# Gate and up projections of a two-layer decoder trunk as 2x2 block products: seven half-width products in place of eight

## The chip, the core and the metric

The kernel runs on one core of a Trainium2 chip. The metric is the device time of one execution in microseconds (us), lower is better. Before the change it is 1854.85 us (median of 3 runs, 1853.87 to 1855.31).

## What is computed

The program is a trunk of two layers over 512 positions of width 1024, all in float32. Each layer is a feed-forward network (FFN), a mixer (a causal convolution beside differential attention), and a second FFN. Only the FFN is touched:

```python
def swiglu(h, w_gate, w_up, w_down):
    return (jax.nn.silu(h @ w_gate) * (h @ w_up)) @ w_down

# per layer, D_MODEL = 1024, D_FF = 2816, SEQ = 512
x = x + 0.5 * swiglu(rms_norm(x, ffn1_norm[l]), ffn1_w_gate[l], ffn1_w_up[l], ffn1_w_down[l])
...
x = x + 0.5 * swiglu(rms_norm(x, ffn2_norm[l]), ffn2_w_gate[l], ffn2_w_up[l], ffn2_w_down[l])
```

So there are four FFNs in one execution.

## The kernel before

**Layout.** Activations are kept transposed: features on the 128 partitions, the 512 positions along the free side. The 1024 input features are 8 tiles `k`; the 2816 hidden features are 22 tiles `m`. TensorE (PE) takes one 128x128 block of a weight as the stationary operand and a 128x512 activation tile as the moving one, and adds into one bank of PSUM (128x512 float32).

**Three matmuls for one product.** Operands are split into a high and a low part in the fp32r type, and `mm3` (L96 to L102) adds three matmuls: high by high (L98), weight-high by activation-low (L101), weight-low by activation-high (L102). `chunk` (L84 to L94) loads 128x1024 of weights by the SP queue (L91), ScalarE (ACT) makes the high part by a copy (L92), VectorE (DVE) makes the low part by a subtraction (L93). The buffers `wraw`, `whi`, `wlo` are rings of 4, 5 and 5 tiles.

**The FFN** (`ffn`, L227). The 22 tiles `m` are done in two halves of 11. For each `m` there is a pair: gate and up, each 8 `k` tiles by 3 matmuls of 512 columns, into two banks that `pair_banks` takes in turn from three pairs of banks. The first two pairs of an FFN run together (`first_products`), since the factor `r` of the RMS norm comes only while they run; `r` (tile `rb`) multiplies the results. DVE multiplies the gate by `r` (L249), ACT takes SiLU (L251), DVE multiplies up by `r` and then by the gate (L253, L254), and ACT and DVE split the result into `hh` and `hl` (L255, L256). After 11 tiles the down projection follows: 8 output tiles by 11 products into a bank `ps_d`, added to `x` at L266.

**Order.** Every engine has its own queue of instructions and runs it in order. The order within a queue is made when the program is built, by a scheduler that works from modelled times; only matmuls that are pinned with `keep_in_program_order` keep the order of the source. Data dependences become semaphore waits.

Of the kernel before, what the change touches and what calls it, by code (L numbers as in the profile page):

```python
# [37 lines left out]
MASK = -1e30  # L38
RLEN = 640
STATS_AT = 5  # L40

SPACE = 392

# [18 lines left out]
def trunk(ctx: ExitStack, tc: tile.TileContext, xt, par, lamv, relb, onehot,  # L62
# [12 lines left out]
    def f32(ap):  # L75
        return ap.bitcast(F32)
# [3 lines left out]
    def bank(tag, name):  # L80
        return psum.tile([P, 512], F32, tag=tag, name=name, bufs=BANKS[tag])


    def chunk(src, eng=None, cuts=1):  # L84
        raw = wp.tile([P, 1024], F32, tag="wraw", name="wraw", bufs=4)
        hi = wp.tile([P, 1024], F32R, tag="whi", name="whi", bufs=5)
        lo = wp.tile([P, 1024], F32R, tag="wlo", name="wlo", bufs=5)
        n = 1024 // cuts
        for c in range(cuts):
            s = slice(c * n, (c + 1) * n)  # L90
            nc.sync.dma_start(raw[:, s], src[:, s])  # L91
            S.activation(hi[:, s], raw[:, s], AF.Copy)  # L92
            (eng or V).tensor_tensor(out=lo[:, s], in0=raw[:, s], in1=f32(hi[:, s]), op=ALU.subtract)  # L93
        return hi, lo  # L94

    def mm3(ps, w, x, start, stop, pin=False):  # L96
        (wh, wl), (xh, xl) = w, x
# [99 lines left out]
    def wpart(w, b, n=P):  # L197
        return w[0][:, b * n : (b + 1) * n], w[1][:, b * n : (b + 1) * n]

    def products(pr, w, ps, i, pin=False):  # L200
        for k in range(KT):
            mm3(ps, wpart(w[i], k), pr[k], k == 0, k == KT - 1, pin=pin and k == 0)

    def first_products(pr, w, ps, early=False):


        if not early:
            rc, v = rows_rstd(pr.s, DM)
# [15 lines left out]
        return [bank(tag, "ps_pair") for _ in range(2)]  # L224


    def ffn(pr, gu, dn, after, lead=None, aside=None):  # L227
        with tc.tile_pool(name="ffn", bufs=1) as fp:
            r = None
            for half in range(2):  # L230
                hh = fp.tile([P, HALF, SEQ], F32R, tag="hh", name="hh")
                hl = fp.tile([P, HALF, SEQ], F32R, tag="hl", name="hl")
                held = []
                for mm in range(HALF):
                    m = half * HALF + mm
                    if m == 4 and aside:
                        aside(fp)
                    w = lead if lead and m == 0 else [chunk(gu[m, 0]), chunk(gu[m, 1])]
                    held.append((mm, w, pair_banks(m)))
                    if m == 0:  # L240
                        continue
                    if m == 1:
                        _, _, r = first_products(pr, [h[1] for h in held], [h[2] for h in held])
                    else:
                        for i in range(2):
                            products(pr, w, held[-1][2][i], i)
                    for n, _, ps in held:
                        gs = fp.tile([P, SEQ], F32, tag="gs", name="gs", bufs=2)
                        V.tensor_tensor(gs, ps[0], r, op=ALU.mult)  # L249
                        sg = fp.tile([P, SEQ], F32, tag="sg", name="sg", bufs=2)  # L250
                        S.activation(sg, gs, AF.Silu)  # L251
                        us = fp.tile([P, SEQ], F32, tag="us", name="us", bufs=2)
                        V.tensor_tensor(us, ps[1], r, op=ALU.mult)  # L253
                        V.tensor_tensor(us, us, sg, op=ALU.mult)  # L254
                        S.activation(hh[:, n, :], us, AF.Copy)  # L255
                        V.tensor_tensor(hl[:, n, :], us, f32(hh[:, n, :]), op=ALU.subtract)  # L256
                    held = []
                w = None
                for m in range(KT):
                    ps = bank("mm", "ps_d")  # L260
                    for kk in range(HALF):
                        b = m * HALF + kk
                        if b % 8 == 0:
                            w = chunk(dn[half, b // 8])
                        mm3(ps, wpart(w, b % 8), (hh[:, kk, :], hl[:, kk, :]), kk == 0, kk == HALF - 1)
                    V.scalar_tensor_tensor(x[:, m, :], ps, 0.5, x[:, m, :], op0=ALU.mult, op1=ALU.add)  # L266
                    if half == 1:
                        after(m)
# [1 line left out]

    bias = const.tile([P, HEADS, SEQ], F32, tag="bias", name="bias")

    def make_bias(bp):
# [3 lines left out]
        oh = bp.tile([NBUCKET + 1, RLEN], F32, tag="oneh", name="oneh", bufs=1)  # L277
        nc.gpsimd.dma_start(oh, onehot)
        row = bp.tile([HEADS, RLEN], F32, tag="brow", name="brow", bufs=1)
        for a, n in ((0, 512), (512, RLEN - 512)):  # L280
            ps = bank("tp", "ps_bias")
            T.matmul(ps[:HEADS, :n], ext, oh[:, a : a + n], start=True, stop=True)
            V.tensor_scalar(row[:, a : a + n], ps[:HEADS, :n], -1.0, None, op0=ALU.mult)
        d1 = dram.tile([HEADS, RLEN], F32, tag="d1", name="d1")
        d2 = dram.tile([HEADS, P, RLEN], F32, tag="d2", name="d2")
        nc.gpsimd.dma_start(d1, row)
# [4 lines left out]

    nlam, gq, gsub, ghalf = [], [], [], []

    def make_scalars(bp):
        for l in range(DEPTH):
            lv = bp.tile([P, 4, HD], F32, tag="lamv", name="lamv", bufs=1)
            nc.gpsimd.dma_start(lv, lamv[l].partition_broadcast(P))
            pr = bp.tile([P, 2, HD], F32, tag="lamp", name="lamp", bufs=1)
# [319 lines left out]
    for k in range(KT):  # L618
        pr.tile(k)

    def aside(bp):
        make_bias(bp)
        make_scalars(bp)

    for l in range(DEPTH):
        nxt = {}
# [89 lines left out]
```

## Time and profile before

| | us |
|---|---|
| median of 3 runs | 1854.85 |
| the profiled execution | 1855.65 |
| its span in the profile | 1852.8 |
| PE busy | 1839.1 (99%) |
| DVE busy | 939.5 (51%) |
| ACT busy | 666.2 (36%) |
| GpSimd (POOL) busy | 343.1 (19%) |
| moved by DMA | 176.21 MB, mean 95 GB/s |

The profile holds one execution. Its page gives the busy time of each engine, the chain of work that ended last, the costliest groups of instructions (line, engine, operation, tiles, shape, count, busy time, mean duration, and what ended the idle time before them), and the DMA issues with the time from issue to landing. A timeline lists single instructions with their start. Matmuls are pipelined, so the duration of one overlaps that of the next, and what one costs is the distance between two starts.

### The profile page before, as it was taken

The page shows a single profiled execution, that of the slowest core. Times are in us where ns is not written, and L with a number is a line of the kernel's source. Part 1 is how long each engine was busy: PE and PEld are TensorE (multiplying, and loading weights), DVE is VectorE, ACT ScalarE, POOL GpSimd, SP SyncE. Part 2 cuts the span into 40 slices and gives each one's busy share as a digit, 9 for nine tenths or more (in the row PEclk, how much of TensorE's full clock was granted, in tenths as well). Part 3 has the DMA queues.
Part 4 walks back from the last instruction along what each step waited for, and adds up shares of the span by engine and source line. Part 5 has one row for each costly group of instructions (what it writes and reads, how often), then busy time and mean ns, then how long its engine had stood idle before and what let it go on. Part 6 is the DMA issues. An engine that isn't in the chain of part 4 may idle for free.

```text
span 1852.8 us, 21101 instructions
## 1 busy us (share of the span) xinstructions
PE 1839.1 (99%) x8388; PEld 1518.5 (82%) x8388; DVE 939.5 (51%) x1356; ACT 666.2 (36%) x950; POOL 343.1 (19%) x238
## 2 busy tenths in 40 slices
PE   8999999999999999999999999999999999999999
PEld 6888888888788888888888888888887888888887
DVE  7443444458867442444454434443688574434441
ACT  5322233346845231232332212233458443212220
POOL 4000000169832000000100000002797320000000
PEclk9999999999999999999999999999999999999999
DMA  6322222222112223222222232222231132222230
GB/s 230 128 102 92 102 91 103 91 91 92 68 47 91 103 91 102 91 102 93 101 91 103 91 103 91 102 91 102 69 110 50 47 114 92 101 93 101 92 113 34
DMA packets 50482, 176.21 MB, mean 95 GB/s; under 512 B 6358, under 2 KB 6502, under 8 KB 50384
## 3 DMA queue, kind: packets, MB, share of 16 engines
q1 hardware_dynamic: 48672, 171.99, 26.8%
q0 software_dynamic: 1568, 2.80, 0.5%
q8 instruction: 65, 1.06, 0.2%
q14 instruction: 33, 0.27, 0.0%
q10 hardware_dynamic: 144, 0.08, 0.0%
HBM read 172.74 MB, written 3.42 MB: 95 GB/s over the span
## 4 chain that ended last, share of the span: by engine, by line
PE 97%; DVE 2%; ACT 0%; DMA 0%; issue 0%
PE ps_pair L98 19%; PE ps_pair L102 19%; PE ps_pair L101 19%; PE ps_d L102 9%; PE ps_d L98 9%; PE ps_d L101 9%; PE ps_pair L383 2%; PE ps_pair L385 2%; PE ps_pair L384 2%; PE ps_out L101 2%; PE ps_out L102 2%; PE ps_out L98 1%; PE ps_sc L501 1%; PE ps_v L415 1%; PE ps_v L413 1%; PE ps_v L414 1%
## 5 line engine op out<-in xcount | busy, mean ns | idle before, releaser
L92 ACT ACTIVATE whi<-wraw 128x1024 fp32r<-128x1024 f32 (+1 forms) x322 | 338.9, 1055 | 908.0 <-PE ps_pair L101 559.4
L98 PE MATMUL ps_pair<-acth,whi 128*128 128x512 f32 x1536 | 599.7, 392 | 5.5 <-ACT whi L92 5.5
L101 PE MATMUL ps_pair<-actl,whi 128*128 128x512 f32 x1536 | 599.8, 390 | 0.0
L102 PE MATMUL ps_pair<-acth,wlo 128*128 128x512 f32 x1536 | 599.3, 390 | 0.0
L93 DVE TENSOR_TENSOR wlo<-wraw,whi 128x1024 fp32r<-128x1024 f32 (+1 forms) x278 | 343.8, 1238 | 196.7 <-ACT whi L92 196.6
L98 PEld LDWEIGHTS ps_pair<-acth,whi 128*128 128x128 f32 x1536 | 289.3, 188 | 67.5 <-ACT whi L92 5.9
L101 PEld LDWEIGHTS ps_pair<-actl,whi 128*128 128x128 f32 x1536 | 289.3, 188 | 60.8 <-issue 0.7
L102 PEld LDWEIGHTS ps_pair<-acth,wlo 128*128 128x128 f32 x1536 | 289.2, 188 | 60.6 <-DVE wlo L93 0.5
L102 PE MATMUL ps_d<-hh,wlo 128*128 128x512 f32 x704 | 274.1, 389 | 0.0
L101 PE MATMUL ps_d<-hl,whi 128*128 128x512 f32 x704 | 274.0, 389 | 0.0
L98 PE MATMUL ps_d<-hh,whi 128*128 128x512 f32 x704 | 272.7, 389 | 0.0
L192 POOL TENSOR_TENSOR ssum<-ssum,sq 128x512 f32<-128x512 f32 x42 | 68.3, 1626 | 1041.8 <-issue 890.8
L253 DVE TENSOR_TENSOR us<-ps_pair,rb 128x512 f32<-128x512 f32 x88 | 60.8, 691 | 261.8 <-PE ps_pair L102 261.8
L249 DVE TENSOR_TENSOR gs<-ps_pair,rb 128x512 f32<-128x512 f32 x88 | 60.8, 691 | 185.7 <-PE ps_pair L102 174.8
L101 PEld LDWEIGHTS ps_d<-hl,whi 128*128 128x128 f32 x704 | 132.2, 188 | 27.4
L102 PEld LDWEIGHTS ps_d<-hh,wlo 128*128 128x128 f32 x704 | 132.2, 188 | 27.4
L98 PEld LDWEIGHTS ps_d<-hh,whi 128*128 128x128 f32 x704 | 132.2, 188 | 27.3
L467 DVE SCALAR_TENSOR_TENSOR ps_y<-u,par,ps_y 128x512 f32<-128x512 f32 x160 | 120.6, 754 | 4.0
L93 POOL TENSOR_TENSOR wlo<-wraw,whi 128x1024 fp32r<-128x1024 f32 x44 | 105.4, 2402 | 29.7 <-ACT whi L92 29.7
L266 DVE SCALAR_TENSOR_TENSOR x<-ps_d,x 128x512 f32<-128x512 f32 x64 | 44.2, 691 | 127.2 <-PE ps_d L102 127.2
L455 POOL TENSOR_TENSOR yp<-yp,prod 128x512 f32<-128x512 f32 x78 | 100.6, 1290 | 8.6 <-ACT prod L454 5.4
L255 ACT ACTIVATE hh<-us 128x512 fp32r<-128x512 f32 x88 | 55.7, 633 | 58.1 <-DVE us L254 58.1
(139 smaller groups left out, 1546.5 us busy)
## 6 DMA issues: line engine op xcount, KB each, us to landing
wraw<-in_gu SPq DMA_DIRECT2D x174, 512.0 KB, 3.2
wraw<-in_dn SPq DMA_DIRECT2D x88, 512.0 KB, 3.2
wraw<-in_wqkv SPq DMA_DIRECT2D x24, 512.0 KB, 3.2
wraw<-in_wag SPq DMA_DIRECT2D x16, 512.0 KB, 3.2
wraw<-in_wout SPq DMA_DIRECT2D x16, 512.0 KB, 3.2
x<-in_xt SPq DMA_DIRECT2D x8, 256.0 KB, 7.1
out<-x SPq DMA_DIRECT2D x8, 256.0 KB, 2.0
d<-d POOLq DMA_DIRECT2D x1, 1280.0 KB, 21.7
```

The lines of the kernel that those rows point to most:

```text
L92: S.activation(hi[:, s], raw[:, s], AF.Copy)
L93: (eng or V).tensor_tensor(out=lo[:, s], in0=raw[:, s], in1=f32(hi[:, s]), op=ALU.subtract)
L98: first = T.matmul(ps, wh, xh, start=start, stop=False)
L101: T.matmul(ps, wh, xl, start=False, stop=False)
L102: T.matmul(ps, wl, xh, start=False, stop=stop)
L192: G.tensor_tensor(self.s, self.s, sq, op=ALU.add)
L249: V.tensor_tensor(gs, ps[0], r, op=ALU.mult)
L253: V.tensor_tensor(us, ps[1], r, op=ALU.mult)
L255: S.activation(hh[:, n, :], us, AF.Copy)
L266: V.scalar_tensor_tensor(x[:, m, :], ps, 0.5, x[:, m, :], op0=ALU.mult, op1=ALU.add)
L455: G.tensor_tensor(yp, yp, p, op=ALU.add)
L467: V.scalar_tensor_tensor(y, us[c][:, t : t + SEQ], pars[l][:, wc + t : wc + t + 1], y, op0=ALU.mult, op1=ALU.add)
```

## The change

For every tile `m` from `PLAIN = 3` on (19 of 22 in each FFN, 76 pairs in all) gate and up are no longer two separate sums. Write the weight pair as a 2x2 block matrix: rows are input features 0 to 511 and 512 to 1023 (`k` 0 to 3 and 4 to 7), columns are gate and up, so the blocks are g1, u1 (upper rows) and g2, u2 (lower rows). Write the activations as 2x2 blocks too: feature halves by position halves (256 columns each), b11, b12, b21, b22. The four blocks of gate and up are then made from seven block products (Winograd's form) in place of eight: each has 4 tiles `k` by 3 matmuls of 256 columns.

- `sums` makes the seven weights: g1, u2, g1+u1, u2+u1, g1+u2+u1, g2, and the sum of all four. The sums are not made by an engine: `add_into` issues a DMA on the POOL queue that reads the addend from DRAM and accumulates into the raw tile that is already on the chip. A raw tile is first split as (g1, u2); then u1 is accumulated into both halves (128x2x512) and the tile is split again; then g1 into the second half (128x512), split; then g2 into the same half (128x512), split. The three accumulations of a pair are called acc1, acc2, acc3 below; the splits in their order A (128x1024), B (128x1024), C1 (128x512), C2 (128x512), and the split of g2 by itself.
- `Halves` makes, once for an FFN, the normalized activations and three differences t2, t3, t4 of their blocks, each in high and low parts, with POOL, DVE and ACT; `settle` rewrites `acth` and `actl` with the normalized activations.
- `seven` runs the seven products. The four quadrants a, d share one bank and c, b the other. After products 1 to 4 ACT copies a finished part out, after products 5, 6 and 7 DVE adds.
- The rings shrink: `wraw` 3, `whi` 4, `wlo` 4, with small rings of 2 for g2. `hh` and `hl` become one tile for each `m`, and the tables of `make_bias` and `make_scalars` move to other buffers.

The core of the diff:

```diff
+PLAIN = 3
+HS = SEQ // 2
...
+    RING = {"wraw": 3, "whi": 4, "wlo": 4, "wraw2": 2, "whi2": 2, "wlo2": 2}
...
+    def parts_of(raw, hi, lo, eng=None):
+        S.activation(hi, raw, AF.Copy)
+        (eng or V).tensor_tensor(out=lo, in0=raw, in1=f32(hi), op=ALU.subtract)
...
+    def add_into(dst, src):
+        nc.gpsimd.dma_start(dst, src, accum_op=ALU.add)
+
+    def sums(g, u):
+        h = slice(0, 512), slice(512, 1024)
+        raw = ring("wraw")
+        nc.sync.dma_start(raw[:, h[0]], g[:, h[0]])
+        nc.sync.dma_start(raw[:, h[1]], u[:, h[1]])
+        w = {}
+        def give(names, t, raw):
+            parts_of(raw, *t)
+            for n, name in enumerate(names):
+                w[name] = tuple(p[:, n * 512 : (n + 1) * 512] for p in t)
+        give(("g1", "u2"), (ring("whi"), ring("wlo")), raw)
+        raw2 = ring("wraw2", 512)
+        nc.sync.dma_start(raw2, g[:, h[1]])
+        add_into(raw.rearrange("p (b c) -> p b c", b=2), u[:, h[0]].unsqueeze(1).broadcast_to([P, 2, 512]))
+        give(("g1u1", "u2u1"), (ring("whi"), ring("wlo")), raw)
+        last = ring("whi"), ring("wlo")
+        add_into(raw[:, h[1]], g[:, h[0]])
+        give(("g1u2u1",), tuple(p[:, h[0]] for p in last), raw[:, h[1]])
+        give(("g2",), (ring("whi2", 512), ring("wlo2", 512)), raw2)
+        add_into(raw[:, h[1]], g[:, h[1]])
+        give(("all",), tuple(p[:, h[1]] for p in last), raw[:, h[1]])
+        return w
...
+    class Halves:
+        def __init__(self, fp, pr, r):
...
+            for j in range(KT // 2):
+                ha, hb = (fp.tile([P, SEQ], F32, tag=f"hh{PLAIN + i}", name="hn") for i in (j, j + KT // 2))
+                for k, h in ((j, ha), (j + KT // 2, hb)):
+                    V.scalar_tensor_tensor(h, x[:, k, :], col(pr.l, pr.gain, k), r, op0=ALU.mult, op1=ALU.mult)
...
+                G.tensor_tensor(t[:, 1], hb[:, b], ha[:, b], op=ALU.subtract)
+                G.tensor_tensor(ha[:, b], ha[:, a], ha[:, b], op=ALU.subtract)
+                V.scalar_tensor_tensor(t[:, 0], ha[:, b], -1.0, hb[:, b], op0=ALU.mult, op1=ALU.subtract)
+                V.scalar_tensor_tensor(t[:, 2], t[:, 0], -1.0, hb[:, a], op0=ALU.mult, op1=ALU.subtract)
+                S.activation(self.th[:, :, j, :], t, AF.Copy)
+                V.tensor_tensor(self.tl[:, :, j, :], t, f32(self.th[:, :, j, :]), op=ALU.subtract)
+        def settle(self):
+            for k, h in self.whole:
+                S.activation(acth[:, k, :], h, AF.Copy)
+                V.tensor_tensor(actl[:, k, :], h, f32(acth[:, k, :]), op=ALU.subtract)
...
+    def seven(halves, w, banks, fp):
+        a, d = banks[0][:, :HS], banks[0][:, HS:]
+        c, b = banks[1][:, :HS], banks[1][:, HS:]
...
+        def go(ps, wt, xt, first=False):
+            at = halves.get(xt)
+            for j in range(KT // 2):
+                (wh, wl), (xh, xl) = wpart(w[wt], j), at(j)
+                for i, (l, r) in enumerate(((wh, xh), (wh, xl), (wl, xh))):
+                    mm = T.matmul(ps, l, r, start=first and i == j == 0, stop=False, skip_group_check=True)
+                    if i == j == 0:
+                        tc.keep_in_program_order(mm)
+        go(a, "g1", "b11", first=True)
+        S.activation(g[:, :HS], a, AF.Copy)
+        go(d, "u2", "t4")
+        S.activation(n[:, :HS], d, AF.Copy)
+        go(c, "u2u1", "t1", first=True)
+        S.activation(n[:, HS:], c, AF.Copy)
+        go(a, "g1u2u1", "t2")
+        S.activation(g[:, HS:], a, AF.Copy)
+        go(b, "g2", "b21")
+        V.tensor_tensor(g[:, :HS], b, g[:, :HS], op=ALU.add)
+        go(c, "all", "b22")
+        V.tensor_tensor(g[:, HS:], c, g[:, HS:], op=ALU.add)
+        S.activation(g, g, AF.Silu)
+        go(a, "g1u1", "t3")
+        V.tensor_tensor(n[:, HS:], a, n[:, HS:], op=ALU.add)
+        V.tensor_tensor(n[:, :HS], a, n[:, :HS], op=ALU.add)
+        V.scalar_tensor_tensor(n, n, -1.0, g, op0=ALU.mult, op1=ALU.mult)
+        return n
...
                 for mm in range(HALF):
...
+                    if m >= PLAIN:
+                        gated(mm, seven(halves, sums(gu[m, 0], gu[m, 1]), pair_banks(m), fp))
+                        continue
```

More of the change, by code (lines that the diff above doesn't have):

```diff
@@ L81, in bank, with ring @@
         return psum.tile([P, 512], F32, tag=tag, name=name, bufs=BANKS[tag])
+    RING = {"wraw": 3, "whi": 4, "wlo": 4, "wraw2": 2, "whi2": 2, "wlo2": 2}
+    def ring(tag, n=1024):
+        dt = F32 if "raw" in tag else F32R
+        return wp.tile([P, n], dt, tag=tag, name=tag, bufs=RING[tag])
+    def parts_of(raw, hi, lo, eng=None):
+        S.activation(hi, raw, AF.Copy)
+        (eng or V).tensor_tensor(out=lo, in0=raw, in1=f32(hi), op=ALU.subtract)
     def chunk(src, eng=None, cuts=1):
-        raw = wp.tile([P, 1024], F32, tag="wraw", name="wraw", bufs=4)
-        hi = wp.tile([P, 1024], F32R, tag="whi", name="whi", bufs=5)
-        lo = wp.tile([P, 1024], F32R, tag="wlo", name="wlo", bufs=5)
+        raw, hi, lo = ring("wraw"), ring("whi"), ring("wlo")
         n = 1024 // cuts
@@ L91, in chunk @@
             nc.sync.dma_start(raw[:, s], src[:, s])
-            S.activation(hi[:, s], raw[:, s], AF.Copy)
-            (eng or V).tensor_tensor(out=lo[:, s], in0=raw[:, s], in1=f32(hi[:, s]), op=ALU.subtract)
+            parts_of(raw[:, s], hi[:, s], lo[:, s], eng)
         return hi, lo
+    def add_into(dst, src):
[22 more added lines that the diff above has]
+        return w
     def mm3(ps, w, x, start, stop, pin=False):
@@ L227, in ffn, with gated @@
     def ffn(pr, gu, dn, after, lead=None, aside=None):
         with tc.tile_pool(name="ffn", bufs=1) as fp:
-            r = None
+            r = halves = None
             for half in range(2):
-                hh = fp.tile([P, HALF, SEQ], F32R, tag="hh", name="hh")
-                hl = fp.tile([P, HALF, SEQ], F32R, tag="hl", name="hl")
+                hh, hl = [], []
                 held = []
+                def gated(n, us):
+                    hi = fp.tile([P, SEQ], F32R, tag=f"hh{n}", name="hh")
+                    if n < PLAIN:
+                        lo = fp.tile([P, SEQ], F32R, tag=f"hl{n}", name="hl")
+                    elif (n - PLAIN) % 2 == 0:
+                        two = fp.tile([P, 2, SEQ], F32R, tag=f"hl{n}", name="hl")
+                        lo = two[:, 0]
+                        hl.append(two[:, 1])
+                    else:
+                        lo = hl.pop()
+                    S.activation(hi, us, AF.Copy)
+                    V.tensor_tensor(lo, us, f32(hi), op=ALU.subtract)
+                    hh.append((hi, lo))
@@ L243, in ffn @@
                         _, _, r = first_products(pr, [h[1] for h in held], [h[2] for h in held])
+                        halves = Halves(fp, pr, r)
                     else:
[L245 to L246 removed]
+                        for k in range(KT):
+                            for i in range(2):
+                                mm3(held[-1][2][i], wpart(w[i], k), pr[k], k == 0, k == KT - 1)
+                    if m == PLAIN - 1:
+                        halves.settle()
                     for n, _, ps in held:
[L248 removed]
+                        gs = fp.tile([P, SEQ], F32, tag="g", name="gs", bufs=2)
                         V.tensor_tensor(gs, ps[0], r, op=ALU.mult)
[L250 to L252 removed]
+                        S.activation(gs, gs, AF.Silu)
+                        us = fp.tile([P, SEQ], F32, tag="n", name="us", bufs=2)
                         V.tensor_tensor(us, ps[1], r, op=ALU.mult)
[L254 to L256 removed]
+                        V.tensor_tensor(us, us, gs, op=ALU.mult)
+                        gated(n, us)
                     held = []
```

46 lines of the change are left out of this document (30 added, 16 removed).

## The prediction

> **What bounds the kernel now.** I read the page first: span, busy times, chain.
>
> ```profile
> span 1852.8 us, 21101 instructions
> PE 1839.1 (99%) x8388; PEld 1518.5 (82%) x8388; DVE 939.5 (51%) x1356; ACT 666.2 (36%) x950; POOL 343.1 (19%) x238
> PE 97%; DVE 2%; ACT 0%; DMA 0%; issue 0%
> ```
>
> PE works 99% of the span and the chain that ended last runs through it for 97%; nothing else binds. Fewer matmul columns are therefore worth their time, as long as PE is still fed. The profiled execution took 1855.65 us, 2.85 more than its span and 0.8 more than the median.
>
> What one matmul costs is the distance of two starts, read from the timeline of PE: 512 columns in a gate and up stretch, 256 columns in the output projection, the only place with that width.
>
> ```profile
> 600.06 0.39 PE L102 MATMUL ps_pair<-acth,wlo 128*128 128x512 f32 x1
> ...
> 603.46 0.39 PE L102 MATMUL ps_pair<-acth,wlo 128*128 128x512 f32 x1
> ...
> 548.41 0.28 PE L98 MATMUL ps_out<-acth,whi 128*128 128x256 f32 x1
> ...
> 560.65 0.28 PE L98 MATMUL ps_out<-acth,whi 128*128 128x256 f32 x1
> ```
>
> 15 steps in 3.40 us are 0.2267 us each; 102 steps in 12.24 us are 0.120 us. Half the width costs 53%.
>
> **Matmuls removed.** A pair had 48 matmuls of 512 columns: 48 x 0.2267 = 10.88 us. It gets 7 x 4 x 3 = 84 of 256: 84 x 0.120 = 10.08 us. That saves 0.80 us a pair, 61 us over 76 pairs, if PE never waits. Seven eighths would have been 1.36; the rest is lost to the narrower matmul.
>
> **Waits between the seven products.** In the built program the first matmul of product 2 waits for ACT's copy after product 1, and that of product 6 for DVE's addition after product 5, since the quadrants a and d, and c and b, lie in one bank. The products are pinned, and within a half nothing else stands in PE's queue between them. Prices of such a hand-over: the end of a matmul to ACT, ACT to PE, PE to DVE, and the two operations at 256 columns (timeline, chain, and groups by shape).
>
> ```profile
> 498.79 0.60 PE L522 MATMUL ps_at<-ident,e 128*128 128x128 f32 x4
> 499.48 0.60 ACT L524 ACTIVATE at<-ps_at 128x512 f32<-128x512 f32 x1 [0.69 <-PE ps_at L522]
> ...
> 4.90 0.53 ACT whi L92
> 5.47 0.80 PE ps_pair L98
> ...
> 1848.57 0.24 PE ps_d L102
> 1848.83 0.69 DVE x L266
> ...
> L524 ACT ACTIVATE at<-ps_at 128x256 f32<-128x256 f32 x8 | 3.0, 378 | 1.0 <-PE ps_at L522 1.0
> L609 DVE TENSOR_TENSOR x<-ps_out,x 128x256 f32<-128x256 f32 x32 | 13.4, 420 | 15.8 <-PE ps_out L102 15.8
> ```
>
> PE ends at 499.39 and ACT starts 0.09 later; ACT to PE is 0.04, PE to DVE 0.02. So after the last matmul of product 1 starts, the next can start 0.28 + 0.09 + 0.38 + 0.04 = 0.79 us later in place of 0.12: 0.67 us lost. For product 6 it is 0.28 + 0.02 + 0.42 + 0.04 = 0.76, so 0.64 lost. PE's own time of a pair is then 10.08 + 1.3 = 11.4 us, already more than the 10.88 of before. The copies after products 2 to 4 have two products, 2.9 us, of cover; without it each would cost the same 0.65.
>
> **The chain of splits and accumulations.** This part decides. ACT's queue in the built program, for one steady pair p:
>
> ```
> L323 Activation g<-ps_pair 128x256         copy after product 1 of p
> L358 Activation hh<-n 128x512              result of p-1
> L94 Activation whi<-wraw 128x512           C1 of p, waits for acc2 of p
> L94 Activation whi<-wraw 128x1024          A of p+1
> L325, L327, L329                           copies after products 2, 3, 4 of p
> L94 Activation whi<-wraw 128x512           C2 of p, waits for acc3 of p
> L94 Activation whi2<-wraw2 128x512         g2 of p+2
> L94 Activation whi<-wraw 128x1024          B of p+1, waits for acc1 of p+1
> L334 Activation g<-g 128x512               SiLU of p
> ```
>
> A of p+1 stands behind C1 of p. C1 of p needs acc2, which may start only when DVE has finished split B; B needs acc1, which may start only when split A is finished. So from one A to the next ACT goes through A, acc1, B, acc2, C1, and no ring, however deep, shortens it. Behind the waiting C1 stand the copies that PE needs, so PE waits as well. Its terms:
>
> ```profile
> L92 ACT ACTIVATE whi<-wraw 128x1024 fp32r<-128x1024 f32 x318 | 336.4, 1060 | 907.1 <-PE ps_pair L101 559.4 <-PE ps_d L101 262.8 <-issue 54.9
> L92 ACT ACTIVATE whi<-wraw 128x512 fp32r<-128x512 f32 x4 | 2.5, 626 | 0.9 <-DMA wraw<-in_gu 0.7
> L93 DVE TENSOR_TENSOR wlo<-wraw,whi 128x1024 fp32r<-128x1024 f32 x274 | 341.0, 1246 | 196.6 <-ACT whi L92 196.6
> L93 DVE TENSOR_TENSOR wlo<-wraw,whi 128x512 fp32r<-128x512 f32 x4 | 2.7, 691 | 0.1
> ```
>
> A: 1.06 + 1.25. B: 1.06 + 0.42 (the addition of product 6 stands ahead of it on DVE) + 1.25. C1's copy: 0.63. Six hand-overs of 0.04 to 0.09: 0.45. Together 6.1 us, and the period of a pair is 6.1 + S, where S = acc1 + acc2, each from issue to landing. S has no row. The nearest are the DMA issues:
>
> ```profile
> wraw<-in_gu SPq DMA_DIRECT2D x174, 512.0 KB, 3.2
> out<-x SPq DMA_DIRECT2D x8, 256.0 KB, 2.0
> bias<-d POOLq DMA_DIRECT2D x1, 1024.0 KB, 6.1
> lamv<-in_lamv POOLq DMA_DIRECT2D x2, 128.0 KB, 5.9
> d<-brow POOLq DMA_DIRECT2D x1, 10.0 KB, 1.8
> ```
>
> acc1 writes 512 KB, acc2 256 KB. From below: plain transfers of the SP queue, 3.2 + 2.0, S = 5.2; nothing lower, as an accumulation moves at least those bytes. On the POOL queue 1.8 us are fixed (10 KB) and (6.1 - 1.8) / 4 = 1.07 us go for each 256 KB: 2.9 and 3.9, S = 6.8 for a plain copy. An accumulation also reads what it adds to; with the data time doubled it is 4.0 and 6.1, S = 10.1. From above: 128 KB took 5.9 us in the crowded start, so 6 to 7 each, S = 13. I take the middle of plain and doubled, S = 8.45, since the start's crowding is gone (DMA engines are some 25% busy in these stretches) but the second read is real.
>
> The Trainium skill, "DMA: Bandwidth & Descriptors", section "Anatomy of one DMA — SWDGE (gpsimd) path", puts a transfer issued by GpSimd at 2.0 us plus its bytes over 436 GB/s. By it S would be 5.8, an estimate, and the period 11.9; the 1024 KB row would be 4.4, and the trace has 6.1.
>
> **The start of each FFN.** `Halves` and `settle` can start only with `r`, while the third pair runs on PE. Timeline of the second FFN of layer 0, and the engines' busy times between the two moments:
>
> ```profile
> 592.10 0.60 ACT L170 ACTIVATE rb<-ps_spread 128x512 f32<-128x512 f32 x1 [3.50 <-PE ps_spread L166]
> 604.57 0.69 DVE L253 TENSOR_TENSOR us<-ps_pair,rb 128x512 f32<-128x512 f32 x1 [3.30 <-PE ps_pair L102]
> 592.73:604.57 11.84, 11.84 (x54) 9.80 (x53) 8.06 (x12) 6.56 (x9) 0.00 (x0) 1.00 0.25 90
> L467 DVE SCALAR_TENSOR_TENSOR ps_y<-u,par,ps_y 128x512 f32<-128x512 f32 x160 | 120.6, 754 | 4.0
> ```
>
> There are 11.8 us, in which DVE already works 8.1 (third busy figure). New on DVE, by the rows above and widths between them: 8 x 0.75 (normalizing), 8 x 0.42 (differences), 8 x 0.69 (low parts of `actl`), 4 x 0.97 (low parts of t, 768 wide) = 18.8 us. Product 2 of the first pair needs the low part of t4, last of these in DVE's queue. 8.1 + 18.8 - 11.8 - 1.4 (product 1) = 13.7: I take 14 us of waiting for each FFN, 56 in all (0 to 80: none, if DVE's idle time before took it up, or with ACT's 8.4 us of new copies in line too).
>
> **Hidden.** POOL's 228 new issues are inside S; on its queue acc1 of p+1 stands behind acc3 of p, which waits for DVE's split C1 of p, and that comes before split A of p+1 on DVE anyway. Its sums for the norm come in other stretches. The SP queue's loads become smaller halves and run ahead by the raw ring. The rings are one shorter for the down projection and mixer: a 1024-wide tile feeds PE for 24 x 0.2267 = 5.4 us against a split of 2.3 and a load of 3.2, so four tiles suffice; without that cover a tile would cost up to 5.5. The factor `r` on gate and up goes away on DVE, which PE does not feel. The moved tables cost nothing.
>
> **The sum.** The first pair of each half (8) is split beforehand, under the third pair or the down projection, and pays only the bank waits, 8 x 1.3 = 10 us. The other 68 pay the period less 10.08. Span: 1852.8 - 61 + 56 + 10 + 68 x (6.1 + 8.45 - 10.08) = 1857.8 + 304 = 2162; with 2.85 outside the span, 2165 us, 17% slower. I call 0.2% (4 us) about the least change that a measurement of this kernel can tell.
>
> **Rivals.**
> *Cheap accumulation*: S of 5.2 to 6.8. For it: HBM and engines are idle enough. Against it: the POOL rows. With S = 5.2 the period would be 11.3, under PE's 11.4, which then decides: 1857.8 + 68 x 1.32 + 2.85 = 1950; with 6.8, 2052. Chance 0.2. The rule of the Trainium skill named above would give 1984 (period 11.9).
> *Dear accumulation*: the add itself sets the pace, S from 10.1 to 15. Against it: no row shows it; for it: no row shows an add at all. 2277 to 2610. Chance 0.22.
> *Faster*: the waits are filled. In the output projection PE runs transposes (L558) between matmuls of other tiles, so PE could stay busy if other matmuls stood in its queue. This decides in favour if the period comes to PE's bare 10.08, which needs S below 4.0 and both bank waits and the starts covered: 1852.8 - 61 + about 20 + 2.85 = 1815. Against it: the pinned order has no other matmuls inside a half, and S has no row under 5.2. Chance 0.05.
> That the change doesn't do what it says is out: the built program has the 84 matmuls for each of 76 pairs.
>
> **How the numbers follow.** My case, S of 6.8 to 10.1, spans 2052 to 2277 and has 0.5; the remaining 0.03 is a result between 1815 and 1950. The range for 8 in 10 is 1975 to 2420: of the cheap case it drops about 0.04, of the dear one about 0.08, and the faster one and that remainder. 2420 is S = 12.2. Faster 0.05, within 0.2% 0.01, slower 0.94.
>
> **What would show it.** In the profile after: PE's share of the chain falls and POOL's DMAs appear in it; products of 256 columns keep starts 0.120 apart; PE idles before L318 for ACT (copies and `whi`) and DVE, with two gaps of about 0.65 in every pair; pairs follow at 14.5 us; `wraw<-in_gu` on the POOL queue lands in about 5 (512 KB) and 3.5 us (256 KB). I am wrong in mechanism if pairs follow at under 11 us, or if the period does not equal 6.1 + S with the S that is measured.

## The result and the profile after

The changed kernel takes 2299.93 us (median of 4 runs, 2292.73 to 2303.21) against 1854.66 us of the kernel before on the same chip: ratio 1.240, interval 1.237 to 1.243. It is 445 us slower; the forecast was 2165, in a range of 1975 to 2420. The time lies above the 2052 to 2277 of the forecast's main case, in the lowest part of its rival *Dear accumulation*.

The profiled execution took 2303.21 us with a span of 2301.1. From its page: the span, the busy times, the granted clock in 40 slices, the two large DMA queues, the chain that ended last by engine and by line.

```profile
span 2301.1 us, 28742 instructions
PE 1940.3 (84%) x11124; PEld 1703.9 (74%) x11124; DVE 1182.6 (51%) x1848; ACT 917.9 (40%) x1532; POOL 595.9 (26%) x500
...
PEclk9799999999998999899998999999999999999899
...
q0 software_dynamic: 44192, 82.51, 22.6%
q1 hardware_dynamic: 59616, 152.07, 21.3%
...
PE 39%; DMA 30%; DVE 13%; issue 6%; ACT 6%; POOL 0%; ACTq 0%; POOLq 0%; SPq 0%; DVEq 0%
```

PE's share of the chain fell from 97% to 39%. DMA, which had none, now carries 30% and DVE 13%; the page's line entry for that DMA is `wraw<-in_gu`, the weight loads and accumulations. PE is busy for 101 us more than before although it has fewer columns to do.

The DMA issues (count, size of one, median time from issue to landing) and the groups that wait:

```profile
wraw<-in_gu SPq DMA_DIRECT2D x232, 256.0 KB, 3.5
...
wraw<-in_gu POOLq DMA_DIRECT2D x76, 512.0 KB, 6.1
wraw<-in_gu POOLq DMA_DIRECT2D x152, 256.0 KB, 4.2
```

```profile
L95 DVE TENSOR_TENSOR wlo<-wraw,whi 128x512 fp32r<-128x512 f32 (+1 forms) x506 | 500.5, 993 | 657.1 <-ACT whi L94 645.4
L94 ACT ACTIVATE whi<-wraw 128x1024 fp32r<-128x1024 f32 (+1 forms) x550 | 467.8, 873 | 891.3 <-DMA wraw<-in_gu 539.9
L107 POOL DMA_DIRECT2D wraw<-in_gu x228 | 223.4, 981 | 1277.1 <-DVE wlo L95 1198.4
```

The three groups wait for each other in a ring: the split's copy on ACT waits 540 us for landings, the low part on DVE waits 645 us for the copy, the next accumulation on POOL waits 1198 us for the low part. From the DMA issues S, acc1 plus acc2, is 6.1 + 4.2 = 10.3 us, and 6.1 + S predicts a period of 16.4 us.

The period itself, from the timeline of ACT in the second half of an FFN (L323 is the copy after product 1; the time in brackets is idle time and what ended it), and the windows between its starts (busy time of PE, PEld, DVE, ACT, POOL with counts, granted clock, DMA share, GB/s):

```profile
990.95 0.38 ACT L323 ACTIVATE g<-ps_pair 128x256 f32<-128x256 f32 x1 [1.95 <-PE ps_pair L318]
993.76 1.58 ACT L94 ACTIVATE whi<-wraw 128x512 fp32r<-128x512 f32 x2 [1.92 <-DMA wraw<-in_gu]
999.62 1.15 ACT L94 ACTIVATE whi<-wraw 128x512 fp32r<-128x512 f32 x2 [1.83 <-DMA wraw<-in_gu]
1003.14 1.06 ACT L94 ACTIVATE whi<-wraw 128x1024 fp32r<-128x1024 f32 x1 [2.37 <-DMA wraw<-in_gu]
1007.60 0.38 ACT L323 ACTIVATE g<-ps_pair 128x256 f32<-128x256 f32 x1 [2.30 <-PE ps_pair L318]
```

```profile
990.95:1007.60 16.65, 12.31 (x84) 11.73 (x84) 7.24 (x12) 6.24 (x12) 2.94 (x3) 0.90 0.57 111
```

16.65 us from pair to pair. The row at 993.76 is C1 and, directly behind it, A of the next pair (two operations in one row): C1 waits for acc2, and A stands behind it. That is the order of ACT's queue on which the forecast rested. Nothing in the window is busy all the time: DMA's share is 0.57, PE works 12.3 us, DVE 7.2. It is a loop of latencies. Of the 68 periods inside the halves one, in the first FFN, is 34.1 us long; DVE waits 10.5 us in it for a small load of the mixer, `lamv` (number 10 below). The other 67 have a median of 16.6 and a mean of 16.1.

The starts of matmuls did not stay 0.120 apart, and the gaps are not the two of 0.65 us that were forecast: in this window PE has steps of 0.81, 1.43 and 2.93 us, where it waits for ACT (L323, L325) and DVE (L331), which stand behind the splits. What follows such pauses is in the last section.

### The profile page after: what moved, and what is told of

It is laid out like the page before. It is cut to its first block, busy times and chain, and to the rows that moved or that the text cites. A ratio compares the mean times of both kernels' runs of the same rounds, so it can differ in the third digit from the quotient of the medians.

```text
span 2301.1 us, 28742 instructions
## 1 busy us (share of the span) xinstructions
PE 1940.3 (84%) x11124; PEld 1703.9 (74%) x11124; DVE 1182.6 (51%) x1848; ACT 917.9 (40%) x1532; POOL 595.9 (26%) x500
## 3 DMA queue, kind: packets, MB, share of 16 engines
q8 instruction: 87, 1.43, 0.2%
## 4 chain that ended last, share of the span: by engine, by line
PE 39%; DMA 30%; DVE 13%; issue 6%; ACT 6%; POOL 0%; ACTq 0%; POOLq 0%; SPq 0%; DVEq 0%
DMA wraw<-in_gu 30%; DVE wlo L95 7%; PE ps_d L138 6%; PE ps_d L142 6%; PE ps_d L141 6%; ACT whi L94 6%; PE ps_pair L318 6%; PE ps_pair L141 2%; PE ps_pair L142 2%; PE ps_pair L138 2%; PE ps_pair L518 1%; PE ps_pair L517 1%; PE ps_pair L516 1%; PE ps_out L141 1%; PE ps_sc L634 1%
## 5 line engine op out<-in xcount | busy, mean ns | idle before, releaser
L95 DVE TENSOR_TENSOR wlo<-wraw,whi 128x512 fp32r<-128x512 f32 (+1 forms) x506 | 500.5, 993 | 657.1 <-ACT whi L94 645.4
L107 POOL DMA_DIRECT2D wraw<-in_gu x228 | 223.4, 981 | 1277.1 <-DVE wlo L95 1198.4
L318 PE MATMUL ps_pair<-acth,whi 128*128 128x256 f32 x1216 | 373.8, 307 | 151.7 <-DVE g L331 138.9
L318 PE MATMUL ps_pair<-th,whi 128*128 128x256 f32 x912 | 293.4, 322 | 158.1 <-ACT n L325 76.7
L318 PE MATMUL ps_pair<-actl,whi 128*128 128x256 f32 x1216 | 367.9, 303 | 10.2 <-DVE actl L295 10.2
L318 PE MATMUL ps_pair<-acth,wlo 128*128 128x256 f32 x1216 | 366.1, 301 | 0.3 <-DVE wlo L95 0.3
L318 PEld LDWEIGHTS ps_pair<-th,whi 128*128 128x128 f32 x912 | 196.3, 215 | 184.8 <-ACT n L325 87.3
L138 PE MATMUL ps_d<-hh,whi 128*128 128x512 f32 x704 | 276.0, 394 | 16.4 <-ACT whi L94 13.8
L318 PE MATMUL ps_pair<-tl,whi 128*128 128x256 f32 x912 | 280.3, 307 | 10.5 <-DVE tl L289 10.5
L318 PE MATMUL ps_pair<-th,wlo 128*128 128x256 f32 x912 | 277.4, 304 | 0.2 <-DVE wlo L95 0.2
L138 PEld LDWEIGHTS ps_d<-hh,whi 128*128 128x128 f32 x704 | 132.5, 188 | 50.9 <-ACT whi L94 18.9
L138 PE MATMUL ps_pair<-acth,whi 128*128 128x512 f32 x320 | 125.6, 397 | 6.0 <-ACT whi L94 6.0
```

The source lines that it names most:

```text
L95: (eng or V).tensor_tensor(out=lo, in0=raw, in1=f32(hi), op=ALU.subtract)
L107: nc.gpsimd.dma_start(dst, src, accum_op=ALU.add)
L138: first = T.matmul(ps, wh, xh, start=start, stop=False)
L318: mm = T.matmul(ps, l, r, start=first and i == j == 0, stop=False, skip_group_check=True)
```

## The experiments

Twelve kernels were run, each timed beside the kernel before. The period is the distance between the starts of the copy after product 1, as above, the median over the periods inside the halves.

**1. The price of the accumulation: plain copies.** One edit in `add_into`:

```diff
-        nc.gpsimd.dma_start(dst, src, accum_op=ALU.add)
+        nc.gpsimd.dma_start(dst, src)
```

> The three POOL transfers of a pair stay, but copy in place of accumulating (the additions are left out). The order of the splits on ACT is as before: A of the next pair behind C1. Chain theory: the period of a pair is 6.1 us plus the two landings S; if the second read is what an accumulation costs, S falls from 10.3 to about 6.8, the period from 16.4 to about 12.9, the time to about 2050 us. Rival, the fixed cost of a POOL issue is most of S: S stays over 9, the time over 2200 us. Rival, PSUM hand-overs and the lowered TensorE clock set the period: no change, 2300 us. In each case period minus S tells whether 6.1 holds.

Measured: 2087.54 us, ratio 1.126 (1.122 to 1.129), period 13.0. The chain and the DMA issues of this kernel's page:

```profile
PE 49%; DMA 19%; DVE 13%; issue 9%; ACT 4%; POOL 0%; POOLq 0%; ACTq 0%; DVEq 0%
...
wraw<-in_gu POOLq DMA_DIRECT2D x76, 512.0 KB, 3.8
wraw<-in_gu POOLq DMA_DIRECT2D x152, 256.0 KB, 3.0
```

S is 6.8 and 6.1 + S = 12.9. The same bytes from the same queue to the same place land 2.3 and 1.2 us sooner when nothing is added; that alone is 212 us of the kernel. The expected time was 37 us too low, the period right within 0.1.

**2. No transfer at all.** `add_into` returns at once:

```diff
-        nc.gpsimd.dma_start(dst, src, accum_op=ALU.add)
+        return
```

> The three accumulating transfers of a pair are left out altogether (the sums are then not sums); all splits and products stay. Chain theory: S = 0, so the chain gives way and TensorE's own 11.4 us for a pair decide: about 1950 us, somewhat more (to 2030) if the order that results has another wait in it. Rival, bank hand-overs or the clock set the period: it stays over 15 us and the time over 2200 us.

Measured: 1993.79 us, ratio 1.075 (1.072 to 1.078), period 11.9; the chain is PE again (PE 83%, DMA 1%). With the transfers gone PE's own time decides. That time is 0.5 us above the forecast's 11.4; its place is in the timeline of PE, the two spots where a matmul start of a pair is more than 0.3 behind the last:

```profile
1207.85 0.28 PE L318 MATMUL ps_pair<-acth,wlo 128*128 128x256 f32 x1
1208.60 0.38 PE L318 MATMUL ps_pair<-th,whi 128*128 128x256 f32 x1 [0.47 <-ACT g L323]
1208.82 0.28 PE L318 MATMUL ps_pair<-tl,whi 128*128 128x256 f32 x1
...
1214.45 0.28 PE L318 MATMUL ps_pair<-acth,wlo 128*128 128x256 f32 x1
1215.32 0.38 PE L318 MATMUL ps_pair<-acth,whi 128*128 128x256 f32 x1 [0.59 <-DVE g L331]
1215.54 0.28 PE L318 MATMUL ps_pair<-actl,whi 128*128 128x256 f32 x1
```

Before products 2 and 6 the steps are 0.75 and 0.87 in place of 0.12, and the step after each is 0.22: 0.73 and 0.85 us lost, 1.58 a pair where the forecast had 1.3. A third spot, with a step of 0.145 and the next of 0.22, loses 0.13. The time is inside the expected 1950 to 2030.

**3. Products in an order that alternates the banks** (a and d lie in one, c and b in the other), with the accumulations left as they are; each product's copy or addition moves with it:

```diff
         go(a, "g1", "b11", first=True)
-        go(d, "u2", "t4")
         go(c, "u2u1", "t1", first=True)
-        go(a, "g1u2u1", "t2")
+        go(d, "u2", "t4")
         go(b, "g2", "b21")
+        go(a, "g1u2u1", "t2")
         go(c, "all", "b22")
         go(a, "g1u1", "t3")
```

> Only the order of the seven products changes, so that neighbours lie in different banks (1 a, 3 c, 2 d, 5 b, 4 a, 6 c, 7 a): every copy or addition has a product of 1.4 us beside it. The chain of splits and accumulations is untouched. Chain theory: the two bank waits of 0.65 us were covered by the longer wait for C1, so the time stays within 30 us of 2300. Rival, the bank waits add to the period: 1.3 us less for each of 76 pairs, about 2200 us.

Measured: 2369.43 us, ratio 1.278 (1.270 to 1.285), period 17.8. Both expectations missed: the waits for banks were to vanish, and the kernel became 69 us slower. The DMA issues of this kernel:

```profile
wraw<-in_gu SPq DMA_DIRECT2D x232, 256.0 KB, 4.8
...
wraw<-in_gu POOLq DMA_DIRECT2D x76, 512.0 KB, 7.7
wraw<-in_gu POOLq DMA_DIRECT2D x152, 256.0 KB, 4.1
```

acc1 went from 6.1 to 7.7, so S = 11.8 and 6.1 + S = 17.9: the formula holds, its S changed. Timelines of POOL, SP's queue and ACT show what acc1 meets:

```profile
984.63 1.19 POOL L107 DMA_DIRECT2D wraw<-in_gu  x1 [0.63 <-DVE wlo L95]
...
985.29 0.33 SPq L125 DMA_DIRECT2D wraw<-in_gu  x1
988.52 0.33 SPq L114 DMA_DIRECT2D wraw<-in_gu  x1
...
992.53 1.06 ACT L94 ACTIVATE whi<-wraw 128x1024 fp32r<-128x1024 f32 x1 [4.76 <-DMA wraw<-in_gu]
```

The load of g2 (L125) is issued 0.7 us after acc1, and split B, which waits for acc1, starts 7.9 us after acc1's issue. Sorted by the first load that the SP queue issues between acc1's issue and its landing: in the 47 pairs in which that comes within 1.5 us, acc1's median is 8.1; where it comes later, 6.4 (16 pairs); without any load, 5.6 (13 pairs). In the changed kernel itself no load comes so early: 6.2 with a later load (62 pairs), 5.6 with none (14). The new order puts the split of g2 next to split A on ACT and so releases that load at the same moment as acc1. That the longer landing goes with the load is shown; what the two share is not.

**4. The same plain copies on SP's queue:**

```diff
-        nc.gpsimd.dma_start(dst, src, accum_op=ALU.add)
+        nc.sync.dma_start(dst, src)
```

> The three transfers are plain copies issued on the SP queue (additions left out). Chain theory: S is that of plain SP loads, 3.5 + 3.2 = 6.7 at most and 5.2 at least, so the period is 11.4 to 12.8 us and the time 1950 to 2045 us. Rival, POOL as issuer costs nothing beside the accumulation: same time as the plain copy on POOL.

Measured: 2041.16 us, ratio 1.101 (1.097 to 1.104), period 12.6, both inside what was expected. The page's issues now mix copies and loads of a size:

```profile
wraw<-in_gu SPq DMA_DIRECT2D x384, 256.0 KB, 3.0
wraw<-in_gu SPq DMA_DIRECT2D x98, 512.0 KB, 3.5
```

The copies alone (the issues of L107) take 3.4 (512 KB) and 2.7 us (256 KB), so S = 6.1 and 6.1 + S = 12.2, 0.4 us under the period. The queue is a small part of the price, 46 us; the addition is the large one, 212 us.

**5. Alternating banks without transfers** (edits 2 and 3 together).

> The three accumulating transfers of a pair are left out (so the summed weights are not sums), and the seven products of a pair are reordered so that no two neighbours use the same pair of bank halves in a way that waits: g1, u2u1, u2, g2, g1u2u1, all, g1u1. With the transfers alone left out the pair took 11.9 us and the kernel 1993.8 us. Theory (with the chain gone the pair is set by TensorE, 10.1 us of matmuls and two waits for a bank of about 0.65 us each): period 10.5 to 10.9 us, 76 x 1.3 = 99 us less, 1895 us (1870 to 1920). Rival (without the chain the pair is set by ScalarE's and VectorE's work on the weights, not by the bank waits): period stays 11.5 to 12 us, 1960 to 2000 us.

Measured: 1868.82 us, ratio 1.007 (1.005 to 1.010), period 10.20. The window of one period (columns as above):

```profile
1194.84:1205.04 10.20, 10.20 (x87) 10.13 (x86) 7.06 (x12) 6.26 (x11) 0.00 (x0) 1.00 0.26 79
```

The time is 1 us under the expected 1870 to 1920 and the period under the expected 10.5 to 10.9: the bank waits were worth more than their 1.3 us. PE is busy through the whole period at full granted clock. The order that cost 69 us beside the accumulations gains 125 us without them, 1.64 a pair. What a wait is worth depends on what binds.

**6. The order of splits on ACT.** All transfers and all arithmetic are there; the code now traces split A and acc1 of pair p+1 before C1 of pair p, and C1 after the second product:

```diff
-    gated(mm, seven(halves, sums(gu[m, 0], gu[m, 1]), pair_banks(m), fp))
+    st = nxt or start(gu[m, 0], gu[m, 1])          # load, A, acc1
+    second(*st)                                    # B, acc2
+    nxt = start(gu[m + 1, 0], gu[m + 1, 1]) if mm + 1 < HALF else None
+    gated(mm, seven(halves, st, pair_banks(m), fp))  # calls third(*st) after product 2
```

> Same transfers, same arithmetic, same product order as the changed kernel; only the order of work: copy A and the first accumulation of pair p+1 are put ahead of copy C1 of pair p on ScalarE and GpSimd, and copy C1 is made after the second product. Theory (the 16.4 us are a chain: first and second landing one after the other, because A of p+1 stands behind C1 of p on ScalarE): the two landings of neighbouring pairs now overlap; the longest loop left holds one large landing (A, its low part, 6.1 us, B, the third sum's copy): 3.1 + 6.1 + about 3 = 12.2 us, or TensorE's 11.9; period 12 to 13.5 us, 68 x (16.1 - 12.7) = 230 us less, 2070 us (2010 to 2130). Rival (the transfers themselves are the limit: the read-and-add traffic of one queue, so they only get longer when they overlap): landings of 8 us and more, period above 15 us, 2220 to 2320 us.

Measured: 2148.75 us, ratio 1.157 (1.149 to 1.166), period 13.7. The DMA issues:

```profile
wraw<-in_gu POOLq DMA_DIRECT2D x76, 512.0 KB, 5.6
wraw<-in_gu POOLq DMA_DIRECT2D x152, 256.0 KB, 5.2
```

S is 10.8, half a microsecond more than in the changed kernel, and yet pairs follow 2.9 us sooner: 6.1 + S would be 16.9. So the two landings no longer stand one behind the other, and it was the order of the work that had put them there: A behind C1 on ACT, and with A the issue of acc1 on POOL, which this edit moves together. The time is 19 us above the range expected (2010 to 2130), the period 0.2 above. What ends ACT's wait before A is now PE, that is, the release of a tile of the ring of four by a product:

```profile
1995.64 1.06 ACT L94 ACTIVATE whi<-wraw 128x1024 fp32r<-128x1024 f32 x1 [1.64 <-PE ps_pair L323]
1998.36 0.63 ACT L94 ACTIVATE whi<-wraw 128x512 fp32r<-128x512 f32 x1 [1.15 <-DMA wraw<-in_gu]
...
2003.66 1.06 ACT L94 ACTIVATE whi<-wraw 128x1024 fp32r<-128x1024 f32 x1 [2.22 <-DMA wraw<-in_gu]
```

A (1995.64) is ahead of C1 (1998.36) and waits for PE; B (2003.66) waits for acc1.

**7. The same with alternating banks.**

> As first_sum_ahead, with the product order g1, u2u1, u2, g2, g1u2u1, all, g1u1. Chain theory: if the loop with one large landing (12.2 us) is the limit, the bank waits that go (1.3 us a pair) are worth little: 2010 to 2090 us, some 30 us under first_sum_ahead; if TensorE is the limit, 1970 us. Rival of contended transfers: above 2220 us, as for first_sum_ahead.

Measured: 2076.23 us, ratio 1.118 (1.113 to 1.123), period 13.3: within the first expectation's bounds, though the reordering brings 73 us rather than the 30 named. Here acc1 keeps 5.6, as in number 6, where in 75 of 76 pairs no load is issued while it runs.

**8. Sums in on-chip memory.** GpSimd adds with `tensor_tensor` from plainly loaded halves; alternating banks; all the arithmetic is there. u1 is loaded into a ring of its own, `s` is the tile `wraws`, and to make room the raw ring of g2 has one tile:

```diff
-        add_into(raw..., u[:, h[0]]...)
+        for n in range(2):
+            G.tensor_tensor(s[:, h[n]], raw[:, h[n]], u1, op=ALU.add)
...
-        add_into(raw[:, h[1]], g[:, h[0]])
+        G.tensor_tensor(raw[:, h[1]], raw[:, h[1]], s[:, h[0]], op=ALU.add)
...
-        add_into(raw[:, h[1]], g[:, h[1]])
+        G.tensor_tensor(raw[:, h[0]], raw[:, h[1]], raw2, op=ALU.add)
```

> The sums of weights are made by GpSimd tensor_tensor in on-chip memory (four 128x512 additions a pair, 1.1 to 1.6 us each by the rows of that engine), from four plain loads on SyncE; no accumulating transfer; product order g1, u2u1, u2, g2, g1u2u1, all, g1u1. All the arithmetic is there. Theory (the loss is the chain of two accumulating landings and the bank waits, not the block products themselves): sums leave the chain, period 10.6 to 11.5 us, 1900 us (1870 to 1950). Rival (GpSimd and VectorE contend, or the additions take the place of the landings in the same chain): 6.1 + 4 x 1.3 = 11.3 us and more on the chain, VectorE's rows longer than before, 1960 to 2060 us.

Measured: 1940.69 us, ratio 1.045 (1.041 to 1.050), period 11.0, within the first expectation. No complete form of the block products that was run is faster by more than 0.5 us (number 12), and it is still slower than the kernel before. Its 0.85 us a pair over number 5 come with longer low parts on DVE, which the rival had named, with a smaller price than it gave: 1918 ns in the mean for the sums in `wraws` against 1262 ns for the other tiles of the same shape:

```profile
L95 DVE TENSOR_TENSOR wlo<-wraw,whi 128x1024 fp32r<-128x1024 f32 x198 | 249.5, 1262 | 115.8 <-ACT whi L94 115.7
L95 DVE TENSOR_TENSOR wlo<-wraws,whi 128x1024 fp32r<-128x1024 f32 x76 | 145.7, 1918 | 38.0 <-ACT whi L94 32.5
```

Of the 76, the 63 that overlap one of GpSimd's additions by more than 0.3 us take 2061 ns in the mean, the other 13 take 1220.

**9 and 10. The start of an FFN**, on top of number 5: first without `settle`, then without `Halves` too (its tiles `th` are filled with copies of x on ACT, the low parts are the same tile).

```diff
-                    if m == PLAIN - 1:
-                        halves.settle()
```

> no_transfer_alternate (transfers left out, alternating banks) with the step at each FFN's start left out that writes the normalised halves back into acth and actl (8 copies on ScalarE, 8 subtractions on VectorE; the products then read un-normalised halves, and the gated result is scaled down so that it stays finite). Theory (a FFN's start is set by VectorE's queue of 16 halves, 8 low parts t and 8 low parts of the settled halves): 8 x 0.68 = 5.4 us less at each of four starts, 1847 us (1838 to 1854). Rival (the settled halves alone are what TensorE waits for, so the whole start goes): 1805 us. Rival (the start is hidden, the loss is spread over the pairs): 1865 to 1870 us.

Measured: 1852.90 us, ratio 0.999 (0.998 to 1.000): 15.9 us less, 4.0 for each FFN, inside the first expectation's bounds.

> no_transfer_alternate with all of the FFN's start left out: no normalised halves, no sums of halves, no low parts and no settling (the products read un-normalised halves and copies of x in their place; the gated result is scaled down so that it stays finite). What is left of the change is seven half-width products of 84 matmuls a pair. Theory (products at 10.2 us against 48 x 0.2267 = 10.9 us before save 76 x 0.68 = 52 us, and four starts cost the 65 us by which no_transfer_alternate misses that): 1803 us (1790 to 1815). Rival (the loss lies in the pairs or at the ends of the FFNs): above 1840 us.

Measured: 1819.46 us, ratio 0.981 (0.978 to 0.984). Another 33.4 us less, 49.4 for the whole start, where 65 had been put down to it; the time is 4 us above the expected range (1790 to 1815) and fits no rival. Most of the missing 16 us lay in one place, a pause of PE in the first FFN (timelines of DVE and PE; number 11 prices it):

```profile
72.12 0.23 DVE L419 TENSOR_TENSOR lamp<-lamv 128x64 f32<-128x64 f32 x1 [9.32 <-DMA lamv<-in_lamv]
...
74.00 0.58 PE L305 MATMUL ps_pair<-acth,whi 128*128 128x256 f32 x1 [10.10 <-DVE g L316]
```

A small load for the mixer stands on POOL's queue right behind the 1280 KB copy `d<-d` (18.0 us to landing). DVE waits for it, and behind that wait stand the sums of the first pairs. The kernel before had no such wait: there both such loads were issued (at 3.4 and 14.4 us) before that copy (at 28.0). In the changed kernel and in all runs so far DVE waits 8.5 to 12.1 us for it.

**11 and 12. That load on SP's queue**, on top of number 10 and of number 8:

```diff
-            nc.gpsimd.dma_start(lv, lamv[l].partition_broadcast(P))
+            nc.sync.dma_start(lv, lamv[l].partition_broadcast(P))
```

> no_start_work (transfers, FFN starts left out) with the two small loads lamv moved from GpSimd's queue to SyncE's. In no_start_work the second lamv was issued right behind the 1.28 MB copy d<-d (18.0 us) on GpSimd's queue, VectorE waited 9.3 us for it with the first pairs' sums queued behind, and TensorE paused 10.1 us. Theory (a one-off of the new order of work, and the last 17 us of the sum 1855 - 52 = 1803): 1803 to 1812 us. Rival (lamv is slow beside d<-d on any queue, or the pause has another cause): 1817 to 1822 us.

Measured: 1809.64 us, ratio 0.976 (0.973 to 0.979): 9.8 us less, as expected.

> pool_sums_alternate, all the arithmetic there, with lamv on SyncE's queue. TensorE paused 9.5 us once behind the wait for lamv there. Theory of the one-off: 1928 to 1934 us. Rival (another wait follows): 1938 to 1943 us.

Measured: 1940.19 us, ratio 1.046 (1.043 to 1.049): no change, the rival's case. DVE's wait for the load fell from 9.6 to 3.0 us, but PE still paused 8.9 in place of 9.5 us at the same spot, for ACT's copy after product 3. The trace shows what holds ACT there:

```profile
91.52 1.06 ACT L94 ACTIVATE whi<-wraws 128x1024 fp32r<-128x1024 f32 x1 [6.72 <-POOL wraws L127]
```

ACT waits 6.7 us for GpSimd's additions. Those stand on POOL's queue behind the issue of `bias<-d`, which waits 16.0 us for the same copy `d<-d` to land. The load was moved away from that copy, the additions were not.

## Why the prediction was right in its mechanism and 6% short

The runs make a ladder. Each step but the alternating banks and the `lamv` wait leaves out one more part of the work, so the kernels from the second row on do not compute the block products:

| kernel | us | this step |
|---|---|---|
| changed | 2299.9 | |
| plain copies for accumulations | 2087.5 | -212.4 |
| no transfers | 1993.8 | -93.7 |
| alternating banks | 1868.8 | -125.0 |
| no FFN starts | 1819.5 | -49.4 |
| the lamv wait gone | 1809.6 | -9.8 |
| before | 1854.7 | |

The steps hold in this order only: alternating the banks is worth -125 us at its place and +69 at the top.

- **Matmuls.** 84 starts 0.120 apart were forecast as 10.08 us and 61 us saved. With nothing in the way a pair took 10.20, which is 52 us: once in a pair one start is 0.144 and the next 0.221 behind the last, 0.12 us more than the sum had. The bare products came out 45 us (2.4%) faster than before; the 7 us between are not traced to a place. Right in kind; at 10.20 the narrower matmuls give back half of the eighth, 0.68 of 1.36 us a pair.
- **Waits for banks.** Forecast 1.3 us a pair, measured 1.58 in the trace and 1.64 from the clock. The step after each wait (0.22 for 0.12) was not in the sum. In the changed kernel the period of 6.1 + S leaves no room for them, as the sum had it for all but the first pairs.
- **The chain.** Period 6.1 + S was forecast, and the forecast called itself wrong in mechanism if the period was not that. It was, within 0.4: 16.6 for 16.4, 17.8 for 17.9, 13.0 for 12.9 and 12.6 for 12.2 in four kernels with S of 10.3, 11.8, 6.8 and 6.1. Putting A and acc1 ahead of C1 broke it (13.7 against 16.9), which shows that the order of the queues is the cause.
- **S, the term that was mis-sized.** The forecast's price of a plain copy, 3.9 + 2.9 = 6.8, was measured as 3.8 + 3.0. Its price with the data time doubled, 6.1 + 4.0 = 10.1, was measured as 6.1 + 4.2 = 10.3 for the accumulation. The step that failed is the choice between these two: "the middle of plain and doubled, S = 8.45". The 1.85 us between that and 10.3, times 68 pairs, are 126 us of the 139 by which the span was short; the rest is a sum of smaller terms of both signs, the two below among them. The accumulations land as the bound with doubled data time had it, and that bound was already worked out; that they read what they add to is not seen by itself in any run. By the rule of the Trainium skill, "DMA: Bandwidth & Descriptors", section "Anatomy of one DMA — SWDGE (gpsimd) path", S is 5.8 (an estimate); the traces have 6.8 for plain copies and 10.3 for accumulations, so the measurement decides here against both the rule and its use for an accumulating DMA.
- **FFN starts.** 56 us were forecast, 49.4 measured where PE binds (the wait for `lamv` in the first FFN stands in both kernels of that step). In the changed kernel it is less: the first period of FFNs 2 to 4 is 19.5, 22.9 and 18.9 against 16.6. The low parts on DVE were the wait, as forecast: the page names `actl` and `tl`, with 10.2 and 10.5 us of PE's time over all four FFNs.

```profile
L318 PE MATMUL ps_pair<-actl,whi 128*128 128x256 f32 x1216 | 367.9, 303 | 10.2 <-DVE actl L295 10.2
L318 PE MATMUL ps_pair<-tl,whi 128*128 128x256 f32 x912 | 280.3, 307 | 10.5 <-DVE tl L289 10.5
```

- **What was called hidden.** "POOL's 228 new issues are inside S" held. "The moved tables cost nothing" did not: the change moved `lamv` behind a long copy, 9.8 us where PE binds, and in the changed kernel the one period of 34.1 us holds that wait; what it costs there was not measured by itself.
- **Rivals.** The measured time is the dear accumulation's: S of 10.1 to 15, 2277 to 2610, chance 0.22, and 2299.9 is at its low end. The mechanism is that of the main case, so the two differ in S alone; that the range held is owed to its having taken in much of this rival. The cheap one needed S up to 6.8, which only a plain copy reaches. The faster one needed S below 4.0 and all else covered; only the kernels that leave work out come near it.

## What to carry to other kernels

Before work is cut on a full engine, follow each new tile through the queues in their order: here two landings that stood one behind the other in an engine's queue set the period, at a DMA share of 0.57, and a reordering was worth 151 us, more than the cut. Start an estimate for an accumulating DMA from a plain one with its data time doubled, which fitted here at 256 and 512 KB, and issue no load right after it. Measure the bare gain first, with everything that feeds it left out: here it was 2.4%, 45 us, and the ladder's five costs of 10 to 212 us had to be hidden to keep it.

## What the runs showed of the hardware

**After pauses of PE the granted clock is lower, and 256-wide matmuls are slower.** Windows of the changed kernel (columns as above) and the timeline of PE after a pause:

```profile
905.00:919.00 14.00, 14.00 (x64) 11.58 (x63) 3.65 (x4) 2.12 (x2) 2.11 (x2) 1.00 0.32 68
919.00:933.00 14.00, 9.28 (x48) 8.41 (x47) 3.12 (x4) 2.86 (x5) 2.05 (x2) 0.77 0.42 80
```

```profile
929.09 0.58 PE L318 MATMUL ps_pair<-th,whi 128*128 128x256 f32 x1 [4.72 <-ACT g L323]
929.47 0.41 PE L318 MATMUL ps_pair<-tl,whi 128*128 128x256 f32 x1
929.68 0.41 PE L318 MATMUL ps_pair<-th,wlo 128*128 128x256 f32 x1
...
933.31 0.33 PE L318 MATMUL ps_pair<-actl,whi 128*128 128x256 f32 x1
933.48 0.28 PE L318 MATMUL ps_pair<-acth,wlo 128*128 128x256 f32 x1
933.59 0.29 PE L318 MATMUL ps_pair<-acth,whi 128*128 128x256 f32 x1
```

After a pause of 4.72 us matmuls start 0.213 us apart in place of 0.120, and do so until 933.3, some 4 us later; the granted clock of the window 926.6 to 933.4 is 0.50. The mean granted clock of the run is 0.942, in the period shown above 0.90, against 1.00 in the kernel before and in number 11, whose PE has no such pauses behind its start. That is part of why PE is busy longer with fewer columns: 872 steps of the products are 0.205 to 0.218 us long, 81 us more than at 0.120. The period fits 6.1 + S without a term for it. The Trainium skill, "TensorE: Matmul & The Clock Gate", section "What's actually happening", has the clock fall to half after an idle window of about 3.4 us and come back after as long a busy one; the trace agrees in the half and in the 4 us, with a ratio of 1.78 in the distances.

**An accumulation lands later when a plain load is issued right after it** (number 3): acc1 took 8.1 us with a 256 KB load issued within 1.5 us after it, 5.6 with none, at a DMA share of some 0.5. **DVE's low parts are longer beside GpSimd's additions** (number 8): 2061 ns for 1220 at 128x1024.
